# Down projection in three passes instead of four, its results added onto residual rows that already lie in the output

## The chip, the cores and the metric

One core of one Trainium2 chip runs the whole program. Times are device microseconds of an execution; a profiled execution has a trace beside its time. TensorE (PE; its weight loads are PEld), VectorE (DVE), ScalarE (ACT), GpSimd (POOL) and SyncE (SP) run their instructions in order, each on its own, and wait for one another by semaphores. DMAs are issued by SP and by POOL and are carried out by the core's 16 DMA engines.

## The reference

One decoder layer in fp32 for 2048 prompt rows of width 1024 and for 32 sample rows (8 requests of 4): a mixer, a cross-attention over a memory, and a feed-forward part, each between two RMS norms. The change lies in the last lines of the last part:

```python
hf = rmsnorm(h, lw['ln_ffn_pre'])
f = (jax.nn.silu(hf @ lw['w_gate']) * (hf @ lw['w_up'])) @ lw['w_down']
h = h + rmsnorm(f, lw['ln_ffn_post'])
```

`w_gate` and `w_up` are 1024 x 2816, `w_down` is 2816 x 1024. What is asked is h of both groups of rows, and the states and memory keys of the parts before.

## The kernel before

From about 860 us on, everything large is one list of passes, and a pass is a list of units: `o` (w_out), `s` (scores), `v` (values), three `g` passes (gate and up, over blocks of 3, 3 and 2 row blocks) and the `d` passes (down). A row block is 256 rows; there are NJ = 8.

A unit of a `d` pass is one row block against one part of w_down. It is computed as seven products instead of eight (sums and differences of the four quarters of the operands are multiplied, and PSUM banks are read in between and then accumulated on). Each product is made of k-tiles of 128, and each k-tile of three matmuls of 128 x 128 by 128 x 512, because both operands are split into an upper half (rounded by ScalarE) and a lower half (the rest, by VectorE). The 22 k-tiles per row are 11 pairs u, and `PARTS` says which pairs a pass takes: 2, 3, 3 and 3. So a product of a pass of n pairs has n x 3 matmuls, and `d` has 11 x 7 x 3 x 8 matmuls in all.

The order in which the products run is `TURN` (0, 1, 3, 2, 5, 4, 6), with product 0 of the next unit ahead of product 6 of this one (`order`). I call such a place in the list a step. In every step the program writes: the product's matmuls, the emptying of its bank (`evac_d`: ACT copies for some products, DVE adds for the others), the upper and lower halves of the moving rows of the step four ahead (`Unit.hi`, on rows `raw` that SP loads from `aT`), one piece of the coming pass's weights where there is one (`Pieces.larger` on ACT, `Pieces.smaller` on DVE), one turn of each pending sequel (`posts`, `tick`), and one turn of a side list (`aux`, by `RATES`). The order of issue on each engine is pinned to the order in which it is written.

The weights of a pass are seven pieces, each the right operand of one product. A piece is loaded in one or two transfers through three staging tiles (`st`, `stage()`), split by ACT and DVE into a ring tile `r0` to `r6`, and the next transfer is issued when a staging tile has been read. In a pass's last unit one transfer's worth is converted per step, and the rest in the first unit of the next pass. Between `d` passes a ring tile `r7` lets two more be converted in the second last unit. Pieces of the `o`, `s` and `v` passes are wide (four k-tiles, `wide`): they use another 4 KB per partition, `e0` to `e6`.

Sums of the passes go through a tensor `yp` in DRAM: `evac_d` stores or accumulates (`accum_op`) each half row block there by a POOL DMA. In the last pass POOL accumulates `yp` into the SBUF tile `y`, `after_down` squares, takes the reciprocal root (`rstd_rows`, one operation of it on POOL), scales (L1730), has POOL accumulate the residual rows from `hX`, and then POOL stores the result. The last two units work otherwise (`after_direct`): their `yp` and `hX` rows are loaded by SP into spare tiles (L2148 to L2153) three units before the end, and DVE adds them.

The samples' rows take part in the gate and up passes as extra columns (`s_f`), and `samples_down` does their down projection as a side list from the first `d` pass on, with weights of its own (44 transfers of 256 KB).

Of the kernel before, what the change touches and what calls it, by code (L numbers as in the profile page):

```python
# [42 lines left out]
def hymba_kernel(ctx: ExitStack, tc: tile.TileContext, a: dict, o: dict, dbg: dict | None = None):  # L43
# [1376 lines left out]
    pg = pd = samp2 = s_f = None  # L1420
# [24 lines left out]
    PARTS = [(0, 2), (2, 3), (5, 3), (8, 3)]  # L1445
# [156 lines left out]
    made, ring = [0], [7, None]  # L1602
    inside, spent = {}, set()

    class Pieces:
# [15 lines left out]
        def larger(self):  # L1621
# [4 lines left out]
            if i not in self.at:  # L1626
                k = made[0] % ring[0]
# [4 lines left out]
                r = (ring[1] if k == 7 else rp).tile([P, 2 * RW], F32R, name=f"r{k}")  # L1632
                if self.wide:

                    e = rx.tile([P, 1024], F32R, name=f"e{k}")
# [139 lines left out]
    def after_rows(j, m, y, ss, ga, x):  # L1775
# [15 lines left out]
        nc.gpsimd.dma_start(out=hX[rows(j, m)], in_=y)  # L1791
# [69 lines left out]

    def evac_gate(sg, w):
# [14 lines left out]
    def evac_up(sg, w, blk, u):  # L1877
# [6 lines left out]
        def ev(name, ps):  # L1884
# [13 lines left out]
            if name == "C21":  # L1898
                nc.gpsimd.dma_start(out=aT[js[0]:js[0] + n, :, u].rearrange("j p c -> p j c"), in_=og.rearrange("p j q c -> p j (q c)"))
        return ev  # L1900

    def after_down(j, m, y):

        add_rows(y, yp[j][:, m * D:(m + 1) * D])
        yield from pause(6)
        ss = small.tile([P, 8], F32, name="sq2", bufs=8)
        for n in range(2):
            nc.scalar.activation(mxt(), half(y)[n], AF.Square, accum_out=ss[:, n:n + 1])
# [8 lines left out]
    def after_direct(j, m, y, ss, h, last):  # L1917

        if not last:
            yield  # L1920
        if last:
            nc.scalar.activation(mxt(), half(y)[0], AF.Square, accum_out=ss[:, 0:1])
            nc.vector.tensor_tensor(half(y)[1], half(y)[1], half(gain["ln_ffn_post"])[1], op=ALU.mult)
            rs = rstd_rows(ss)
            nc.vector.tensor_tensor(half(y)[0], half(y)[0], half(gain["ln_ffn_post"])[0], op=ALU.mult)
            for n in (1, 0):
                t = half(y)[n]
                nc.vector.scalar_tensor_tensor(t, t, rs[:, 0:1], h[n], op0=ALU.mult, op1=ALU.add)
                nc.sync.dma_start(out=o["y"][rows(j, m), n * 512:(n + 1) * 512], in_=t)
            return  # L1930
        rs = rstd_rows(ss)
        yield
        scaled(y, rs, gain["ln_ffn_post"])
        nc.vector.tensor_tensor(y, y, h, op=ALU.add)
        nc.sync.dma_start(out=o["y"][rows(j, m)], in_=y)

    def evac_d(p, j, z, h, last):

        y = {}
        final = p == len(PARTS) - 1  # L1940
        ss = [small.tile([P, 8], F32, name="sq2", bufs=8) for _ in range(2)] if z else None

        def ev(name, ps):
            m, n = divmod(AT[KEEP.get(name, name)], 2)
            if m not in y:
                y[m] = pd.tile([P, D], F32, name="y", bufs=7)
# [10 lines left out]
            end = last and name == "C21"  # L1957
            if z and not end:
                later.append(lambda: nc.scalar.activation(mxt(), t, AF.Square, accum_out=ss[m][:, n:n + 1]))
            if name in ("C12", "C21"):  # L1960
                if z:
                    posts.append(after_direct(j, m, y[m], ss[m], h[m], end))
                elif final:
                    posts.append(after_down(j, m, y[m]))
# [4 lines left out]
    def samples_down():  # L1969

        m = pd.tile([P, D], F32, name="m")[:NS]
        ss = small.tile([P, 8], F32, name="s_sq", bufs=1)
        for n in range(2):
            ps = mxt()

            for k0 in range(0, FT, 4):
                ws = []
                for kt in range(k0, min(k0 + 4, FT)):
                    ws.append(pd.tile([P, 512], F32, name="w", bufs=4))
                    nc.sync.dma_start(out=ws[-1], in_=a["w_down"][n, kt // 2, :, (kt % 2) * 512:(kt % 2 + 1) * 512])  # L1980
                yield from pause(5)
                for g, w in enumerate(ws):
                    kt = k0 + g
                    nc.tensor.matmul(ps[32 * g:32 * g + 32], lhsT=s_f[:, kt].rearrange("p h t -> p (h t)"), rhs=w,
                                     start=kt < 4, stop=kt >= FT - 4, tile_position=(0, 32 * g))
                yield
            t = m[:, n * 512:(n + 1) * 512]
# [3 lines left out]
            yield  # L1991
            nc.vector.tensor_tensor(t, t, half(gain["ln_ffn_post"])[n][:NS], op=ALU.mult)
            yield
        h = pd.tile([P, D], F32, name="y", bufs=7)[:NS]
# [13 lines left out]
    RATES = {"o": (0, 9), "s": (0, 9), "v": (0, 0), "g": (6, 4), "d": (0, 8)}  # L2008
# [23 lines left out]
    def enter(k):  # L2032
# [13 lines left out]
        if kind == "g":  # L2046
            if i == 0:
                rctx.close()
                pg = fctx.enter_context(tc.tile_pool(name="pg", bufs=1, reuse_waits="tile"))
# [256 lines left out]
```

## Time and profile before

| | us |
|---|---|
| median of 3 runs | 2885.15 (2884.6 to 2893.62) |
| profiled execution, its own time | 2880.55 |
| its span, first to last instruction | 2878.6 |
| `d` passes, from the first 128 x 512 matmul after the gate stage (2381) to the end | 497 |

In a table by stretches each engine's busy time stands with the number of its instructions, PEclk is the share of full TensorE clock that was granted in that stretch, and DMA the mean busy share of the 16 engines. Idle time of an engine costs only where TensorE waits for it.

### The profile page before, as it was taken

The numbers are of one execution on the slowest core, as the hardware profiler recorded it, in microseconds if no ns is written. First come the engines' busy times: TensorE is split into PE (matmuls) and PEld (weight loads), VectorE is DVE, ScalarE is ACT, GpSimd is POOL, SyncE is SP. The second block draws the span as 40 slices with busy tenths as digits, with TensorE's granted clock in tenths as the row PEclk, the third lists the DMA queues.
The fourth block names the chain that finished last, engine by engine and source line by source line (L and its number), as shares of the span: only waits on it lengthen the run. The fifth ranks groups of instructions, "written<-read, shape, count | busy, mean of one in ns | idle before, by whom it ended". The sixth has DMA issues, their size and how long they took to land. (4 is left out here: it accounts for less than half of the span.)

```text
span 2878.6 us, 42299 instructions
## 1 busy us (share of the span) xinstructions
PE 2762.0 (96%) x15207; PEld 2369.9 (82%) x15207; DVE 2083.5 (72%) x3915; ACT 1523.0 (53%) x3045; POOL 556.6 (19%) x754
## 2 busy tenths in 40 slices
PE   8999999999988999999899999999999999899996
PEld 8888787787866878878798988889999997677774
DVE  7677677776737887777887787677678886655665
ACT  5545553644446786777754534434455554444452
POOL 2142342321321321025312100001000000011122
PEclk9999999999999999999999999999999999999998
DMA  7345535342256885568855567763243347877787
GB/s 250 117 138 183 150 109 158 107 150 87 78 200 232 278 293 200 173 193 244 270 187 203 172 237 265 244 229 129 106 145 133 125 140 229 249 168 172 177 215 229
DMA packets 161137, 530.02 MB, mean 184 GB/s; under 512 B 19408, under 2 KB 30848, under 8 KB 149408
## 3 DMA queue, kind: packets, MB, share of 16 engines
q1 hardware_dynamic: 99504, 331.81, 35.7%
q0 software_dynamic: 49184, 170.52, 19.2%
q10 hardware_dynamic: 12240, 24.99, 2.6%
q8 instruction: 120, 1.97, 0.3%
q14 instruction: 89, 0.73, 0.1%
HBM read 373.10 MB, written 154.15 MB: 183 GB/s over the span
## 5 line engine op out<-in xcount | busy, mean ns | idle before, releaser
L134 PE MATMUL accA<-r,s 128*128 128x512 f32 (+2 forms) x1792 | 641.9, 358 | 42.3 <-DVE y L1954 12.0
L136 PE MATMUL accA<-r,s 128*128 128x512 f32 (+2 forms) x1792 | 631.8, 353 | 1.9 <-DVE s L1574 1.8
L135 PE MATMUL accA<-r,s 128*128 128x384 f32 (+2 forms) x1600 | 556.2, 348 | 2.0 <-DVE r L1645 2.0
L134 PEld LDWEIGHTS accA<-r,s 128*128 128x128 f32 x1792 | 341.2, 190 | 100.1 <-ACT s L1572 20.9
L1572 ACT ACTIVATE s<-sum 128x512 fp32r<-128x512 f32 (+2 forms) x488 | 289.1, 593 | 233.9 <-DVE sum L1554 105.2
L136 PEld LDWEIGHTS accA<-r,s 128*128 128x128 f32 x1792 | 341.1, 190 | 34.0 <-DVE s L1574 3.4
L134 PE MATMUL accC<-r,s 128*128 128x512 f32 (+2 forms) x896 | 320.9, 358 | 19.2 <-ACT y L1952 7.9
L135 PEld LDWEIGHTS accA<-r,s 128*128 128x128 f32 x1600 | 304.8, 190 | 25.6 <-DVE r L1645 4.6
L1574 DVE TENSOR_TENSOR s<-sum,s 128x512 fp32r<-128x512 f32 (+2 forms) x488 | 310.7, 644 | 20.1 <-ACT s L1572 18.8
L136 PE MATMUL accC<-r,s 128*128 128x512 f32 (+2 forms) x896 | 315.2, 352 | 0.4 <-DVE s L1574 0.3
L1574 DVE TENSOR_TENSOR s<-raw,s 128x512 fp32r<-128x512 f32 (+2 forms) x366 | 234.5, 641 | 71.6 <-ACT s L1572 69.4
L135 PE MATMUL accC<-r,s 128*128 128x384 f32 (+2 forms) x800 | 277.0, 346 | 0.3 <-DVE r L1645 0.3
L1572 ACT ACTIVATE s<-raw 128x512 fp32r<-128x512 f32 (+2 forms) x366 | 218.2, 596 | 67.5 <-PE accC L136 50.0
L128 ACT ACTIVATE whi<-wraw 128x1024 fp32r<-128x1024 f32 (+2 forms) x148 | 137.1, 940 | 186.3 <-PE acc L135 98.4
L134 PEld LDWEIGHTS accC<-r,s 128*128 128x128 f32 x896 | 169.9, 190 | 50.6 <-issue 12.0
L129 DVE TENSOR_TENSOR wlo<-wraw,whi 128x1024 fp32r<-128x1024 f32 (+2 forms) x148 | 163.1, 1112 | 64.3 <-ACT whi L128 63.6
L136 PEld LDWEIGHTS accC<-r,s 128*128 128x128 f32 x896 | 170.0, 190 | 16.6 <-DVE s L1574 1.5
L134 PE MATMUL acc<-xh,whi 128*128 128x512 f32 (+1 forms) x464 | 168.5, 364 | 8.4 <-ACT xh L289 8.2
L142 POOL TENSOR_TENSOR rs<-ms,nhalf 128x1 f32<-128x1 f32 (+4 forms) x125 | 114.9, 920 | 317.9 <-DVE ms L140 301.6
L136 PE MATMUL acc<-xh,wlo 128*128 128x512 f32 (+1 forms) x464 | 164.6, 356 | 1.7 <-DVE wlo L129 1.7
L135 PE MATMUL acc<-xl,whi 128*128 128x512 f32 (+1 forms) x464 | 164.3, 355 | 0.2 <-DVE xl L290 0.2
L135 PEld LDWEIGHTS accC<-r,s 128*128 128x128 f32 x800 | 152.0, 190 | 10.8 <-DVE r L1645 0.6
(649 smaller groups left out, 5835.9 us busy)
## 6 DMA issues: line engine op xcount, KB each, us to landing
raw<-in_w_gu_dram SPq DMA_DIRECT2D x66, 1024.0 KB, 5.0
wraw<-in_w_in_fm_dram SPq DMA_DIRECT2D x52, 512.0 KB, 3.6
wraw<-in_w_in_tm_dram SPq DMA_DIRECT2D x48, 512.0 KB, 3.7
yp<-y POOLq DMA_DIRECT2D x48, 512.0 KB, 7.3
raw<-aT SPq DMA_DIRECT2D x24, 768.0 KB, 5.1
st<-in_w_down_dram SPq DMA_DIRECT2D x34, 512.0 KB, 6.4
aT<-og POOLq DMA_DIRECT2D x22, 768.0 KB, 4.1
hX<-y POOLq DMA_DIRECT2D x32, 512.0 KB, 6.6
```

The lines of the kernel that those rows point to most:

```text
L128: last[0] = nc.scalar.activation(hi[:, cs], raw[:, cs], AF.Copy)
L129: nc.vector.tensor_tensor(lo[:, cs], raw[:, cs], f(hi)[:, cs], op=ALU.subtract)
L134: nc.tensor.matmul(ps, lhsT=wh, rhs=ah, start=start, stop=False, skip_group_check=more)
L135: nc.tensor.matmul(ps, lhsT=wh, rhs=al, start=False, stop=False, skip_group_check=more)
L136: nc.tensor.matmul(ps, lhsT=wl, rhs=ah, start=False, stop=stop, skip_group_check=more)
L142: nc.gpsimd.tensor_tensor(out=rs[:rows, :cols], in0=ms[:rows, :cols], in1=nhalf[:rows, :cols], op=ALU.pow)
L1572: nc.scalar.activation(h3, v, AF.Copy)
L1574: return lambda: nc.vector.tensor_tensor(l3, v, f(h3), op=ALU.subtract)
```

## The change

- `PARTS` becomes 3, 4 and 4 pairs: three `d` passes instead of four, the last two with wide pieces (16 KB per partition with both halves), whose `e` tiles come from a new pool `rd`, opened before the last gate pass. The ring is seven tiles throughout; `r7` and the two early pieces are gone.
- In the value pass the residual rows are stored to the output `y` itself instead of `hX`, for all row blocks but the last. In the last `d` pass the result is accumulated there by one POOL DMA.
- In the last pass the tiles `y` begin as rows of `yp`, which SP loads one unit ahead; every bank is then emptied by a DVE add. Nothing is accumulated into SBUF any more.
- Only the last unit reads residual rows into staging tiles (`after_last`).
- `samples_down` joins the side list in the last gate pass, loads 22 transfers of 512 KB into `e` tiles, and waits for the columns `s_f` that a product needs (`there`).

```diff
-    PARTS = [(0, 2), (2, 3), (5, 3), (8, 3)]
+    PARTS = [(0, 3), (3, 4), (7, 4)]
...
-        nc.gpsimd.dma_start(out=hX[rows(j, m)], in_=y)
+
+        nc.gpsimd.dma_start(out=(hX if x is not None or j + 1 == NJ else o["y"])[rows(j, m)], in_=y)
...
-        add_rows(y, yp[j][:, m * D:(m + 1) * D])
-        yield from pause(6)
...
-        add_rows(y, hX[rows(j, m)])
-        yield from pause(5)
-        nc.gpsimd.dma_start(out=o["y"][rows(j, m)], in_=y)
...
+        yield
+        nc.gpsimd.dma_start(out=o["y"][rows(j, m)], in_=y, accum_op=ALU.add)
...
+    def after_last(j, m, y, ss, h):
+
+        hy, ga = half(y), half(gain["ln_ffn_post"])
+        if m == 0:
+            nc.vector.tensor_tensor(hy[0], hy[0], ga[0], op=ALU.mult)
+            yield
+            nc.vector.tensor_tensor(hy[1], hy[1], ga[1], op=ALU.mult)
+        else:
+            nc.scalar.activation(mxt(), hy[0], AF.Square, accum_out=ss[:, 0:1])
+            nc.vector.tensor_tensor(hy[0], hy[0], ga[0], op=ALU.mult)
         rs = rstd_rows(ss)
...
+        for n in (1, 0):
+            nc.vector.scalar_tensor_tensor(hy[n], hy[n], rs[:, 0:1], half(h)[n], op0=ALU.mult, op1=ALU.add)
+            nc.sync.dma_start(out=o["y"][rows(j, m), n * 512:(n + 1) * 512], in_=hy[n])
...
-            if name in KEEP or name == "C21":
-                if z:
-                    nc.vector.tensor_tensor(t, ps, half(z[m])[n], op=ALU.add)
-                else:
-                    nc.scalar.copy(t, ps)
+            if not final and (name in KEEP or name == "C21"):
+                nc.scalar.copy(t, ps)
             else:
                 nc.vector.tensor_tensor(t, ps, t, op=ALU.add)
...
+                    w = f(rd.tile([P, 1024], F32R, name=f"e{2 * (i % 3) + c}"))
+                    nc.sync.dma_start(out=w, in_=a["w_down"][n, u])
...
+            while us[-1] >= there[0]:
                 yield
...
-    RATES = {"o": (0, 9), "s": (0, 9), "v": (0, 0), "g": (6, 4), "d": (0, 8)}
+    RATES = {"o": (0, 9), "s": (0, 9), "v": (0, 0), "g": (6, 4), "d": (0, 10)}
...
+            if i + 1 == len(BLOCKS):
+                aux.append(samples_down())
...
+        if i == 2 and n + 1 < len(work) and passes[work[n + 1][0]][:2] == ("d", len(PARTS) - 1):
+
+            ys[n + 1] = {}
+            for m in range(2):
+                ys[n + 1][m] = pd.tile([P, D], F32, name="y", bufs=6)
+                nc.sync.dma_start(out=ys[n + 1][m], in_=yp[work[n + 1][1]][:, m * D:(m + 1) * D])
...
-        p = coming if work[cur][2] == 1 or coming and kind == "d" and work[cur][2] == 2 and i in (5, 4) else now if begins[cur] else None
+        p = coming if work[cur][2] == 1 else now if begins[cur] else None
```

SP's order at the program's end before: five units' `aT` rows, then the last two units' addends, then the last unit's `aT` rows, then stores.

```order
L1595 DMA raw<-aT 128x1536 x5
L2148 DMA r_27114<-yp 128x1024
L2153 DMA r_27114<-hX 128x1024
L2148 DMA r_27114<-yp 128x1024
L2153 DMA m<-hX 128x1024
L2148 DMA st<-yp 128x1024
L2153 DMA st<-hX 128x1024
L2148 DMA st<-yp 128x1024
L2151 DMA w<-hX 128x512 x2
L1595 DMA raw<-aT 128x1536
L1935 DMA out_y_dram<-y 128x1024 x3
L1929 DMA out_y_dram<-y 128x512 x2
```

The same place now: one pair of `yp` rows per unit, between the `aT` rows, and the residual rows of the last unit only.

```order
L2169 DMA y<-yp 128x1024 x2
L1599 DMA raw<-aT 128x2048
L2169 DMA y<-yp 128x1024 x2
L1599 DMA raw<-aT 128x2048
L2169 DMA y<-yp 128x1024 x2
L2157 DMA st<-hX 128x1024 x2
L1934 DMA out_y_dram<-y 128x512 x4
```

The eight addends no longer stand ahead of the last `aT` rows, and no `aT` load is left behind the last two pairs.

POOL in the last pass before, for two half row blocks:

```order
L1721 DMA y<-yp 128x1024
L1721 DMA y<-hX 128x1024
L1915 DMA out_y_dram<-y 128x1024
L142 TENSOR_TENSOR rs<-ms,nhalf 128x1
L1721 DMA y<-yp 128x1024
L1721 DMA y<-hX 128x1024
L1915 DMA out_y_dram<-y 128x1024
L142 TENSOR_TENSOR rs<-ms,nhalf 128x1
```

And now, for two half row blocks:

```order
L142 TENSOR_TENSOR rs<-ms,nhalf 128x1
L1919 DMA out_y_dram<-y 128x1024
L142 TENSOR_TENSOR rs<-ms,nhalf 128x1
L1919 DMA out_y_dram<-y 128x1024
```

Of three POOL DMAs per half row block one is left; it accumulates.

DVE at the end of the program now (`y<-acc` empties a bank; L1925, L1927, L1930 and L1954 multiply by the gain; L1933 closes a row half):

```order
L1949 TENSOR_TENSOR y<-accC,y 128x512
L1925 TENSOR_TENSOR y<-y,ga 128x512
L1949 TENSOR_TENSOR y<-accA,y 128x512
L1954 TENSOR_TENSOR y<-y,ga 128x512
L1927 TENSOR_TENSOR y<-y,ga 128x512
L1729 TENSOR_TENSOR sq_27100<-sq_26966 128x1
L140 TENSOR_SCALAR ms<-sq_27100 128x1
L1933 SCALAR_TENSOR_TENSOR y<-y,rs,st 128x512 x2
L1949 TENSOR_TENSOR y<-accA,y 128x512
L1930 TENSOR_TENSOR y<-y,ga 128x512
```

The first half row block's closing operations stand before the add that empties the last bank.

## Rows read from the trace of the kernel before

**Rows 1.** The page's head and its first part: busy time, share of the span and instructions of an engine.

```profile
span 2878.6 us, 42299 instructions
PE 2762.0 (96%) x15207; PEld 2369.9 (82%) x15207; DVE 2083.5 (72%) x3915; ACT 1523.0 (53%) x3045; POOL 556.6 (19%) x754
```

**Rows 2.** The table by stretches: stretch and its length, busy time of each engine (instructions), granted clock, DMA share, GB/s. In this order: entry into the `d` passes, their three changes of pass, the inside of the last pass, its last three units, the tail, the inside of the `o` pass, the changes from `o` to `s` and from `s` to `v`.

```profile
2360.00:2392.00 32.00, 27.37 (x160) 24.53 (x158) 26.73 (x50) 18.29 (x34) 1.28 (x2) 0.89 0.58 192
2452.00:2490.00 38.00, 30.27 (x117) 22.60 (x115) 27.44 (x46) 21.66 (x40) 2.13 (x4) 0.87 0.79 272
2580.00:2622.00 42.00, 34.75 (x138) 26.96 (x138) 29.41 (x46) 23.12 (x39) 3.46 (x4) 0.93 0.77 203
2716.00:2746.00 30.00, 24.18 (x102) 18.40 (x101) 19.89 (x32) 16.42 (x28) 1.79 (x3) 1.00 0.78 216
2746.00:2820.00 74.00, 74.00 (x328) 61.21 (x327) 52.06 (x102) 39.23 (x93) 25.55 (x35) 1.00 0.96 238
2820.00:2868.60 48.60, 32.87 (x122) 24.74 (x120) 27.49 (x51) 13.58 (x37) 10.97 (x16) 0.89 0.79 224
2868.60:2878.60 10.00, 0.00 (x0) 0.00 (x0) 5.95 (x9) 0.72 (x2) 0.87 (x1) 0.66 0.36 144
905.00:1040.00 135.00, 134.89 (x643) 112.04 (x642) 106.41 (x186) 99.64 (x214) 43.30 (x67) 1.00 0.76 264
1040.00:1080.00 40.00, 36.56 (x164) 29.31 (x164) 36.70 (x53) 34.42 (x65) 10.22 (x12) 0.96 0.90 305
1232.00:1250.00 18.00, 16.01 (x71) 12.07 (x70) 14.44 (x23) 14.93 (x33) 2.02 (x3) 1.00 0.46 167
```

**Rows 3.** Waits of TensorE from 2381 us to the end: who waited for whom, us in total, times, longest.

```profile
PE accA L134 <- DVE y L1954: 12.0, 5, 5.4
PE accC L134 <- ACT y L1952: 7.9, 5, 3.3
```

**Rows 4.** ScalarE's upper halves of weight pieces (L1641), 2440 to 2746 us: its idle time before them, by what ended it (us, times).

```profile
  DMA st<-wT: 22.8, 14
  DMA st<-in_w_down_dram: 8.3, 3
```

**Rows 5.** The chain that ended last, in order of time, near the end: start, us, what.

```profile
2816.73 26.16 DMA raw<-aT
2842.99 0.53 ACT s L1572
```

**Rows 6.** DMA from 2740 us to the end: queues with packets, MB and share of the 16 engines (q0 is POOL's, q1 SP's), then issues with their count, KB each and median us to landing.

```profile
q0 software_dynamic: 5222, 18.97, 59.1%
q1 hardware_dynamic: 3051, 11.33, 22.6%
...
y<-yp POOLq DMA_DIRECT2D x12, 512.0 KB, 8.7
y<-hX POOLq DMA_DIRECT2D x12, 512.0 KB, 8.3
out_y_dram<-y POOLq DMA_DIRECT2D x12, 512.0 KB, 8.7
raw<-aT SPq DMA_DIRECT2D x6, 768.0 KB, 7.1
...
st<-yp SPq DMA_DIRECT2D x2, 512.0 KB, 24.9
```

**Rows 7.** The timeline of TensorE at a group of the samples' matmuls: start, us, engine, line, operation, tiles, shape, count.

```profile
2392.07 1.06 PE L1984 MATMUL mx<-w,s_f 128*32 128x512 f32 x8
```

**Rows 8.** VectorE's timeline where the samples' rows are closed.

```profile
2582.16 1.27 DVE L1232 SCALAR_TENSOR_TENSOR m<-m,rs,y 32x1024 f32<-32x1024 f32 x1 [4.34 <-DMA y<-hXs]
```

**Rows 9.** DMA issues of 2452 to 2490 us: count, KB each, median us to landing.

```profile
st<-wT SPq DMA_DIRECT2D x4, 512.0 KB, 6.8
...
st<-wT SPq DMA_DIRECT2D x4, 256.0 KB, 4.4
```

**Rows 10.** Groups of VectorE's instructions inside the `o` pass, 905 to 1040 us: line, operation, tiles, shapes, count, busy us, mean ns of one, idle before.

```profile
L1574 DVE TENSOR_TENSOR s<-sum,s 128x512 fp32r<-128x512 f32 x26 | 17.8, 686 | 0.6 <-ACT s L1572 0.6
L1730 DVE SCALAR_TENSOR_TENSOR y<-y,rs,ga 128x1024 f32<-128x1024 f32 x13 | 16.6, 1277 | 0.0
...
L1554 DVE TENSOR_TENSOR sum<-raw 128x512 f32<-128x512 f32 x12 | 8.3, 688 | 0.2
L1750 DVE TENSOR_TENSOR y<-accB,y 128x512 f32<-128x512 f32 x7 | 4.8, 691 | 4.1 <-PE accB L136 4.1
```

**Rows 11.** The timeline of the tail, the last product of TensorE first.

```profile
2866.30 0.47 PE L134 MATMUL accA<-r,s 128*128 128x512 f32 x1 [0.88 <-DVE sq L1725]
...
2868.20 0.39 PE L136 MATMUL accA<-r,s 128*128 128x512 f32 x1
2868.62 0.69 DVE L1950 TENSOR_TENSOR y<-accA,st 128x512 f32<-128x512 f32 x1 [2.22 <-PE accA L136]
2869.23 1.28 DVE L1730 SCALAR_TENSOR_TENSOR y<-y,rs,ga 128x1024 f32<-128x1024 f32 x1
...
2870.54 1.23 DVE L1934 TENSOR_TENSOR y<-y,st 128x1024 f32<-128x1024 f32 x1
...
2872.78 0.87 POOL L142 TENSOR_TENSOR rs<-ms,nhalf 128x1 f32<-128x1 f32 x1 [5.08 <-DVE ms L140]
2873.69 1.42 DVE L1928 SCALAR_TENSOR_TENSOR y<-y,rs,w 128x512 f32<-128x512 f32 x2 [0.47 <-POOL rs L142]
```

More of the change, by code (lines that the diff above doesn't have):

```diff
@@ L1418, in hymba_kernel, with rooms4 @@
     RW = 1536
[L1420 removed]
+    pg = pd = samp2 = s_f = rd = None
+    def rooms4():
+        return rd or rx
     posts = []
@@ L1859, in after_values @@
         put(4, u, 0)
+    there = [0]
     def evac_gate(sg, w):
@@ L1898, in ev, with after_down @@
             if name == "C21":
+                if w > n * P:
+                    there[0] = u + 1
                 nc.gpsimd.dma_start(out=aT[js[0]:js[0] + n, :, u].rearrange("j p c -> p j c"), in_=og.rearrange("p j q c -> p j (q c)"))
         return ev
-    def after_down(j, m, y):
-        add_rows(y, yp[j][:, m * D:(m + 1) * D])
-        yield from pause(6)
-        ss = small.tile([P, 8], F32, name="sq2", bufs=8)
-        for n in range(2):
-            nc.scalar.activation(mxt(), half(y)[n], AF.Square, accum_out=ss[:, n:n + 1])
+    def after_down(j, m, y, ss):
         yield
@@ L1912, in after_down, with evac_d @@
         scaled(y, rs, gain["ln_ffn_post"])
-        add_rows(y, hX[rows(j, m)])
-        yield from pause(5)
-        nc.gpsimd.dma_start(out=o["y"][rows(j, m)], in_=y)
-    def after_direct(j, m, y, ss, h, last):
-        if not last:
-            yield
[L1921 to L1930, printed above, removed]
-        rs = rstd_rows(ss)
[L1932 to L1939, printed above, removed]
+        yield
[4 more added lines that the diff above has]
+            nc.vector.tensor_tensor(hy[0], hy[0], ga[0], op=ALU.mult)
+            yield
+            nc.vector.tensor_tensor(hy[1], hy[1], ga[1], op=ALU.mult)
+        else:
+            nc.scalar.activation(mxt(), hy[0], AF.Square, accum_out=ss[:, 0:1])
+            nc.vector.tensor_tensor(hy[0], hy[0], ga[0], op=ALU.mult)
+        rs = rstd_rows(ss)
+        for n in (1, 0):
+            nc.vector.scalar_tensor_tensor(hy[n], hy[n], rs[:, 0:1], half(h)[n], op0=ALU.mult, op1=ALU.add)
+            nc.sync.dma_start(out=o["y"][rows(j, m), n * 512:(n + 1) * 512], in_=hy[n])
+    def evac_d(p, j, y, h):
         final = p == len(PARTS) - 1
-        ss = [small.tile([P, 8], F32, name="sq2", bufs=8) for _ in range(2)] if z else None
+        ss = [small.tile([P, 8], F32, name="sq2", bufs=8) for _ in range(2)] if final else None
         def ev(name, ps):
@@ L1956, in ev @@
                 return
-            end = last and name == "C21"
-            if z and not end:
+            if h and name == "C22":
+                nc.scalar.activation(mxt(), t, AF.Square, accum_out=ss[m][:, n:n + 1])
+                nc.vector.tensor_tensor(t, t, half(gain["ln_ffn_post"])[n], op=ALU.mult)
+            elif final and not (h and name == "C21"):
                 later.append(lambda: nc.scalar.activation(mxt(), t, AF.Square, accum_out=ss[m][:, n:n + 1]))
             if name in ("C12", "C21"):
-                if z:
-                    posts.append(after_direct(j, m, y[m], ss[m], h[m], end))
+                if h:
+                    posts.append(after_last(j, m, y[m], ss[m], h[m]))
                 elif final:
-                    posts.append(after_down(j, m, y[m]))
+                    posts.append(after_down(j, m, y[m], ss[m]))
                 else:
@@ L2078, in before_loads @@
     def before_loads(k):
+        nonlocal rd
         kind, i, _ = passes[k]
-        if kind != "d":
+        if kind != "g" or i + 1 < len(BLOCKS):
             drain(aux)
```

87 lines of the change are left out of this document (42 added, 45 removed).

## The prediction

> **What bounds the kernel now.** I read the page's head first: TensorE is busy 2762.0 of 2878.6 us [rows 1], so the time can only fall where TensorE stands still or runs at half clock. The change touches the last projection, so next came a table by stretches of it [rows 2]. The stretch 2746 to 2820, inside a pass, is solid: 74.00 us busy of 74 at clock 1.00. The stretches around the four changes of weights and the end are not. I price each as its length less busy time times granted clock, since a busy microsecond at the lower level (1.2 of 2.4 GHz) does half the work:
>
> entry from the gate stage, 2360 to 2392: 32 - 27.37 x 0.89 = 7.6 us;
> first change of pass, 2452 to 2490: 38 - 30.27 x 0.87 = 11.7;
> second, 2580 to 2622: 42 - 34.75 x 0.93 = 9.7;
> third, 2716 to 2746: 30 - 24.18 = 5.8;
> last three units, 2820 to 2868.6: 48.6 - 32.87 x 0.89 = 19.3;
> tail without a matmul: 10.0.
>
> Together 64.1 us. Then the waits of TensorE in that stage [rows 3]: at changes of pass it waits for VectorE and ScalarE to empty PSUM (12.0 and 7.9 us), and those stand behind weight pieces that have not landed: ScalarE idled 22.8 and 8.3 us before a piece's upper half [rows 4]. Near the end it is one transfer: the last unit's aT rows, issued at 2816.73, landed 26.16 us later [rows 5], where the median of its kind is 7.1 us [rows 6].
>
> Why 26 us: over 2740 to 2879 the software queue (POOL's DMAs) holds the 16 engines 59.1% and the hardware queue 22.6% [rows 6]. That is 82.1 us for 36 POOL transfers of 512 KB, 2.28 us each, and 31.4 us for 11.33 MB, 1.45 us per 512 KB. A unit of the last pass there takes two reads of yp, two of hX and two writes, all POOL's, and 768 KB of aT: 6 x 2.28 + 1.5 x 1.45 = 15.9 us of DMA. It has 7 x 9 matmuls; with 74 us for 328 of them [rows 2], 0.226 us each, that is 14.2 us. The pass asks more of the DMA engines than it lasts, the backlog grows, and the two units' addends loaded ahead of the last aT rows (24.9 us to landing, rows 6) meet it.
>
> **The change part by part.**
> The matmuls stay: 11 x 7 x 3 x 8 = 1848, 417 us, however they are cut. So do the samples' 44: a group of four holds TensorE 1.06 us [rows 7], and by the order of instructions 4 of 12 groups move into the gate stage and the rest into the first pass. Neutral there; they no longer end beside the second change of pass, where VectorE stood 4.34 us for hXs [rows 8]. What they may cost now (a fold in the first unit, the same hXs wait in the first pass at 2.0-us steps): 0 to 4 us, taken as 1, as a step's bank wait hides most of it.
>
> One change of pass goes. The three left each convert 14 pieces, seven of them in the last unit of the pass before, with three in flight.
> Entry: now 14 pieces (512 and 256 KB) instead of 7, but one step later each product needs two. The seven done ahead cover the first three products; after that the steps shrink from 2.7 to 2.0 us. Bounds 5 (the third change now, of the same shape with a start two steps earlier, 5.8) and 12 (the first, 11.7); I take 7, near the entry of now.
> First change, three to four units deep: the outgoing unit's steps are 2.0 us as now, the incoming 2.7. Bounds 4.9 (the change from w_out to the wide scores' weights, 40 - 36.56 x 0.96, the same wide pieces) and 11.7; I take 6, nearer to the wide one, because a wide piece's 512 KB takes 6.8 us [rows 9], and three in flight on 2.7-us steps cover 8.1.
> Second, wide to wide: the attention stage does it twice, at 4.9 and 2.0 us [rows 2]; upper bound the 9.7 of today. I take 4.
>
> The end: a unit of the last pass now moves 1 MB of aT, two loads of yp on SP's queue and two accumulating stores: 2 x 2.28 + 4 x 1.45 = 10.4 us of DMA in 7 x 12 x 0.226 = 19.0 us, 55% instead of 112%. With no backlog the aT rows land in about the 7.1 us of their kind and nothing else is late: VectorE, which takes over the adds that ScalarE's copies did, has 7 adds of 0.69, 7 lower halves of 0.69, 4 sums of 0.69 and 2 scalings of 1.28 [rows 10], 15.0 us of 19.0. The first attention pass, 905 to 1040, ran the same steps with VectorE busy 106.41 of 135 us (79%) and TensorE 134.89 [rows 2]: such a load hides. What is left of 19.3 us: bounds 0 and 10 (half of it, if the adds delay PSUM), taken as 1.5, mostly the last product's wait for its bank, 0.88 us now [rows 11].
> POOL loses 24 accumulating loads and 16 yp stores; it is on no path but the one above. The moved residual rows (hX to the output) are the same store.
>
> Tail: of today's 10.0 us, VectorE's scaling and addend of another row half (1.28 and 1.23) stand before the final row [rows 11]. After, the other half's two closing operations (1.42 for both) stand before the last PSUM add instead, and one gain product has been done earlier. From the last matmul: add 1.9, square 2.8, POOL's power 4.2, two closing operations 5.7, then 3.5 from there to the end as now: 9.3. Bounds 7 and 10.
>
> Sum of what stays: 1 + 7 + 6 + 4 + 1.5 + 9.3 = 28.8, so 64.1 - 28.8 = 35.3 us are saved: 2880.55 - 35 = 2845 for the profiled execution. The median shown, 2885.15, is 4.6 above that execution; the forecast is 2846. With all low bounds (0, 5, 4.9, 2, 0, 7) 18.9 stay: 2835. With all high ones (4, 12, 11.7, 9.7, 10, 10) 57.4 stay: 2874, and 2878 on the median's footing.
>
> A rule against the change: the Trainium skill, Perfetto Trace Analysis, DMA Optimizations, says that smaller transfers may let some work start sooner. The trace agrees in part: 256-KB pieces land in 4.4 us, 512-KB ones in 6.8 [rows 9]. By it the wider pieces would make each change of pass late, which is the first rival.
>
> **The rivals.**
> First: the changes of pass keep their price (12 + 11.7 + 9.7 instead of 17): every piece is 512 KB, 2.4 us later than half of today's, and ScalarE, in order, holds PSUM copies behind it. Against it the attention stage, with the same pieces at 4.9 and 2.0. Time 2846 + 16 = 2862.
> Second: VectorE bounds the last pass. In the two steps of a unit that hold a scaling it has 0.69 + 0.69 + 0.69 + 1.28 = 3.35 us against 2.7; if no other step gives it back, 0.65 x 2 x 8 = 10 us: 2856. Against it 905 to 1040, with two whole-row operations per half.
> Third, slower: the rows' six buffers are three units; the load for a unit waits until the accumulating store three units before has landed, and SP's queue, with the next aT rows behind it, waits too. From that store's issue (the fifth step of the following unit) to the use there are ten steps, 27 us, of which the load takes some 8.7: it decides when a store takes over 18 us. The median is 8.7 [rows 6], but 24.9 and 26 us have been seen in this pass. At 31 us five units wait 13 us each: 2846 + 65 = 2911.
> Fourth, no change: the backlog stays (the stores are still POOL's, and weights and rows now meet in one place) and the changes of pass keep their price: 2846 + 16 + 18 = 2880.
>
> **How the numbers follow.** Forecast 0.62 (its own range 2835 to 2858), first rival 0.17, second 0.08, fourth 0.07, slower 0.06. The range 2833 to 2868 takes in the first two rivals. A change under 0.3% (8.7 us) can't be told from none: faster 0.87, same 0.07, slower 0.06.
>
> **What would show it.** Three changes of pass, each losing under 8 us, after stretches at clock 1.00; aT rows of the last unit landing under 10 us; no DMA slice at 99% through the last pass; TensorE solid there with VectorE near 80%. It is wrong if TensorE waits for y's adds in every unit of the last pass, if SP waits for accumulating stores, or if ScalarE's idle time before pieces stays at 31 us.

## The result and the profile after

The changed kernel's median is 2856.2 us over 4 runs (2854.98 to 2863.87); the kernel before, timed beside it, 2884.88 (2883.42 to 2893.62). The ratio is 0.99, interval 0.9874 to 0.9926: 28.7 us less, where 39 were forecast; the time lies inside the range of 2833 to 2868. The profiled execution has a span of 2853.3 us instead of 2878.6.

The page's head after:

```profile
span 2853.3 us, 41834 instructions
PE 2757.0 (97%) x15207; PEld 2362.4 (83%) x15207; DVE 2074.9 (73%) x3820; ACT 1486.6 (52%) x2926; POOL 526.2 (18%) x716
```

TensorE has the same 15207 matmuls as in [rows 1] and is busy 5 us less, at a mean granted clock of 0.99 instead of 0.986; most of the gain is idle time that has gone.

The table by stretches after, columns as in [rows 2]: entry into the `d` passes, the fold of the samples' sums in the first unit, first change of pass, second change, inside of the last pass, last units, tail.

```profile
2372.00:2405.00 33.00, 27.77 (x167) 24.43 (x168) 26.64 (x48) 19.73 (x36) 0.71 (x1) 0.90 0.63 212
2470.00:2490.00 20.00, 18.73 (x83) 15.15 (x82) 13.74 (x25) 7.06 (x15) 2.20 (x4) 1.00 0.32 105
2518.00:2545.00 27.00, 25.32 (x107) 19.48 (x106) 24.43 (x32) 17.43 (x25) 1.94 (x3) 1.00 0.84 274
2684.00:2714.00 30.00, 25.45 (x97) 19.68 (x96) 21.73 (x31) 12.77 (x22) 1.43 (x2) 0.89 0.76 235
2714.00:2835.00 121.00, 121.00 (x525) 98.27 (x525) 89.78 (x152) 42.77 (x94) 18.47 (x26) 1.00 0.62 151
2801.00:2843.00 42.00, 41.13 (x179) 33.13 (x177) 30.26 (x52) 13.35 (x30) 5.76 (x9) 1.00 0.51 123
2843.30:2853.30 10.00, 0.33 (x2) 0.00 (x0) 4.34 (x8) 0.72 (x2) 0.76 (x2) 0.66 0.28 106
```

Priced as in the prediction (length less busy time times clock):

| place | before | forecast | after |
|---|---|---|---|
| entry | 7.6 | 7 | 8.0 |
| samples' fold | - | 1 | 1.3 |
| changes of pass | 11.7, 9.7, 5.8 | 6, 4 | 1.7, 7.3 |
| last units | 19.3 | 1.5 | 0.9 |
| tail | 10.0 | 9.3 | 9.7 |
| sum | 64.1 | 28.8 | 28.9 |

(The tail is counted from the end of the last matmul, as before; its row begins 0.33 us ahead of that.) The largest entry went: the last units lose 0.9 us instead of 19.3.

TensorE's waits after, 2381 us to the end, as in [rows 3]:

```profile
PE accA L134 <- DVE t L1902: 4.7, 1, 4.7
PE accC L134 <- ACT s L1576: 3.8, 1, 3.8
PE accA L134 <- DVE y L1949: 1.9, 2, 1.0
```

The first is the entry, the second the second change of pass; the third, two waits of at most 1.0, is all that TensorE waits for the adds into `y`. The 12.0 and 7.9 us of before are gone.

The DMA from 2714 us to the end, queues and issues as in [rows 6]:

```profile
q0 software_dynamic: 1986, 7.22, 33.4%
q1 hardware_dynamic: 3024, 12.58, 25.1%
...
out_y_dram<-y POOLq DMA_DIRECT2D x13, 512.0 KB, 5.5
raw<-aT SPq DMA_DIRECT2D x5, 1024.0 KB, 5.1
y<-yp SPq DMA_DIRECT2D x10, 512.0 KB, 6.5
```

POOL's queue holds a third of the engines instead of 59.1%, and `aT` rows of 1 MB land in 5.1 us, where the last 768 KB of before took 26.16 [rows 5].

Why the trace's own gain is 25.3 and not 35 is seen at one landmark, the first matmul that waits at the entry of the `d` passes (TensorE's timeline). Before:

```profile
2378.36 0.59 PE L134 MATMUL accA<-r,s 128*128 128x272 f32 x1 [4.13 <-DVE t L1894]
```

After:

```profile
2391.48 0.59 PE L134 MATMUL accA<-r,s 128*128 128x272 f32 x1 [4.73 <-DVE t L1902]
```

From there to the end the kernel is 500.2 - 461.8 = 38.4 us shorter, but it arrives there 13.1 us later, and 38.4 - 13.1 = 25.3. Of the 13.1, 0.6 is the longer wait in the bracket, and 5.0 had gathered by the 9000th matmul, ahead of the last gate pass. The other 7.5 come from the samples' four groups that moved there. Counted between the same neighbouring matmuls in both kernels, the groups' slots are 1.4, 2.9, 2.9 and 1.2 us, 8.4 together, of which 0.9 is won back elsewhere in that stage. The two long ones have a wait of this kind (the same timeline, after):

```profile
2234.02 1.05 PE L1993 MATMUL mx<-e,s_f 128*32 128x512 f32 x2 [0.67 <-DVE s_f L1905]
```

The group asks for columns `s_f` that VectorE writes in the same step. The wait is 0.67 us, and the last product then runs 1.05 us by itself instead of beside the other three: such a place costs 1.7 us more than a slot of 1.2.

### The profile page after: what moved, and what is told of

The parts are those of the page before. It is cut to its first block, busy times and chain, and to the rows that moved or that the text cites. A ratio compares the mean times of both kernels' runs of the same rounds, so it can differ in the third digit from the quotient of the medians.

```text
span 2853.3 us, 41834 instructions
## 1 busy us (share of the span) xinstructions
PE 2757.0 (97%) x15207; PEld 2362.4 (83%) x15207; DVE 2074.9 (73%) x3820; ACT 1486.6 (52%) x2926; POOL 526.2 (18%) x716
## 5 line engine op out<-in xcount | busy, mean ns | idle before, releaser
L135 PE MATMUL accA<-r,s 128*128 128x384 f32 (+2 forms) x1472 | 504.8, 343 | 1.9 <-DVE r L1649 1.9
L134 PEld LDWEIGHTS accA<-r,s 128*128 128x128 f32 x1792 | 340.6, 190 | 86.3 <-issue 17.7
L1576 ACT ACTIVATE s<-sum 128x512 fp32r<-128x512 f32 (+1 forms) x456 | 282.3, 620 | 217.1 <-DVE sum L1558 92.1
L136 PEld LDWEIGHTS accA<-r,s 128*128 128x128 f32 x1792 | 340.2, 190 | 34.2 <-DVE s L1578 2.8
L1578 DVE TENSOR_TENSOR s<-sum,s 128x512 fp32r<-128x512 f32 (+1 forms) x456 | 305.6, 677 | 21.6 <-ACT s L1576 21.2
L135 PEld LDWEIGHTS accA<-r,s 128*128 128x128 f32 x1472 | 280.2, 190 | 21.3 <-DVE r L1649 5.0
L1578 DVE TENSOR_TENSOR s<-raw,s 128x512 fp32r<-128x512 f32 (+1 forms) x342 | 232.3, 679 | 52.5 <-ACT s L1576 50.7
L1576 ACT ACTIVATE s<-raw 128x512 fp32r<-128x512 f32 (+1 forms) x342 | 213.3, 624 | 72.0 <-PE accC L136 53.8
L135 PE MATMUL accC<-r,s 128*128 128x384 f32 (+2 forms) x736 | 250.5, 340 | 0.3 <-DVE r L1649 0.3
L134 PEld LDWEIGHTS accC<-r,s 128*128 128x128 f32 x896 | 168.9, 189 | 37.4 <-ACT sg L1877 5.3
L136 PEld LDWEIGHTS accC<-r,s 128*128 128x128 f32 x896 | 169.1, 189 | 16.2 <-DVE s L1578 0.9
L134 PE MATMUL accB<-r,s 128*128 128x512 f32 (+2 forms) x448 | 157.6, 352 | 0.0
```

Source lines behind the costliest of these rows:

```text
L134: nc.tensor.matmul(ps, lhsT=wh, rhs=ah, start=start, stop=False, skip_group_check=more)
L135: nc.tensor.matmul(ps, lhsT=wh, rhs=al, start=False, stop=False, skip_group_check=more)
L136: nc.tensor.matmul(ps, lhsT=wl, rhs=ah, start=False, stop=stop, skip_group_check=more)
L1576: nc.scalar.activation(h3, v, AF.Copy)
L1578: return lambda: nc.vector.tensor_tensor(l3, v, f(h3), op=ALU.subtract)
```

## The experiments

Two questions were open: what had made the end stall, and what of the gain belongs to which part of the change. My reading after the result was that the eight addends of the last two units, issued by SP in one burst onto nearly full DMA engines, made the stall, and that the fewer passes are a gain of their own. The rival was the prediction's own cause: the last pass asks for more DMA than it lasts, so a backlog grows whatever stands at its end.

SP's timeline of the kernel before, near the end:

```profile
2801.96 0.32 SPq L1595 DMA_DIRECT2D raw<-aT  x1
2802.39 0.67 SPq L2148 DMA_DIRECT2D r<-yp  x1
...
2809.37 4.12 SPq L2151 DMA_DIRECT2D w<-hX  x2
2816.73 0.32 SPq L1595 DMA_DIRECT2D raw<-aT  x1
```

The DMA issues of the kernel before from 2746 to 2802, ahead of the burst (count, KB each, median us to landing):

```profile
y<-yp POOLq DMA_DIRECT2D x8, 512.0 KB, 8.1
raw<-aT SPq DMA_DIRECT2D x5, 768.0 KB, 6.8
```

The `aT` rows land after 5.1, 4.2, 6.8, 7.5 and 7.4 us in turn, and POOL's twelve transfers from 2774 to 2802 after 7.9 to 9.0. The times rise once, when POOL's sums begin, and then stay: no backlog grows. The burst's transfers then land after 10.8, 13.6, 15.8 and so on up to 27.6 us, and the `aT` rows behind them after 26.16.

**The changed kernel once more** (after_again), nothing edited.

> The changed kernel unchanged, as the mark that the variants of this batch are compared with, and for a second trace of it. In its first trace the passes ahead of the gate stage, where no instruction differs, ran 5 us later than in the trace of before. If that is chance between executions, the second trace has another figure (-3 to +3 us); if the change of addresses or of the residual rows' destination makes it, it is 4 to 6 us again. Time 2852 to 2860 either way.

Measured: 2854.55 us median of 5, ratio 0.9906 (0.989 to 0.9922), span 2850.7. The landmark stands at 2388.71, so the `d` passes take 462.0 us, as in the first trace to 0.2. At the 9000th matmul this trace is 1.7 us behind that of before, where the first was 5.0: these 3.3 us are chance between executions of one kernel. Whether the remaining 1.7 are is open, as there is one trace of before; the other variants stood between 1.1 ahead of it (four_pool) and 8.2 behind (extra_four) at that place. One thing in these traces speaks against chance alone. From the 6000th matmul (1152 us) to the 9000th, the ten traces of kernels that store residual rows to `y` fall back by 1.3 to 3.3 us against the trace of before, and the two of kernels that store them to `hX` as before (pool_sums, four_pool) by -1.1 and 0.0. The new destination may thus cost some 2 us; no run changes it alone, so that isn't shown.

**Four passes again** (four_passes), with the rest of the change.

```diff
-    PARTS = [(0, 3), (3, 4), (7, 4)]
+    PARTS = [(0, 2), (2, 3), (5, 3), (8, 3)]
```

> PARTS as before (2, 3, 3, 3), everything else of the change kept: one change of pass more, none wide. Theory (the four entries and changes cost 34.8 us in the trace of before by length less busy time times clock, and 17.0 now, so about half of what the change gains comes from them; the end costs under 2 us whatever the number of passes, since a unit of the last pass would take 2 x 2.28 + 3.5 x 1.45 = 9.6 us of DMA in 14.2): 13 to 19 us slower than the changed kernel, 2869 to 2875. Rival (the end made the whole gain, the changes of pass move with other things): within 4 us of the changed kernel.

Measured: 2870.26 us, ratio 0.9958 (0.9944 to 0.9972): 15.7 us above the changed kernel timed beside it. Its waits of TensorE in the `d` passes:

```profile
PE accC L134 <- ACT r L1645: 8.8, 1, 8.8
PE accA L134 <- DVE y L1949: 6.9, 5, 2.1
PE accC L134 <- ACT y L1947: 6.0, 3, 4.4
```

These are the changes of pass: the last alone holds 8.8 us. With the rest of the change in place the three passes are worth some 16 us, and the other parts together with four passes some 12 (0.42%).

**POOL sums the last pass again** (pool_sums): three passes, but `yp` and `hX` are accumulated into `y` by POOL as before, and rows are loaded ahead for the last unit alone, so without a burst.

```diff
+        add_rows(y, yp[j][:, m * D:(m + 1) * D])
+        yield from pause(4)
...
-        nc.gpsimd.dma_start(out=o["y"][rows(j, m)], in_=y, accum_op=ALU.add)
+        add_rows(y, hX[rows(j, m)])
+        yield from pause(3)
+        nc.gpsimd.dma_start(out=o["y"][rows(j, m)], in_=y)
```

> Three passes as in the change, but in the last pass POOL accumulates yp and then hX into y and stores y, as before; only the last unit has its yp rows loaded ahead, as in the change. The two pauses of the sequel are 4 and 3 steps (6 and 5 before), since the steps are longer and there are six tiles y. A unit then asks 6 x 2.28 + 2 x 1.45 = 16.6 us of DMA in 19.0, 87%. Theory (the stall at the end came from a DMA demand above 100%): no stall of 19 us comes back; 0 to 6 us slower than the changed kernel, the last units' aT rows land in 6 to 12 us. Rival (POOL's way through SBUF itself makes the end late, whatever the load): 15 to 25 us slower, with the wait near the end.

Measured: 2855.7 us, ratio 0.9903 (0.989 to 0.9917), no different from the changed kernel. Its table by stretches from the last pass on:

```profile
2714.00:2800.00 86.00, 86.00 (x373) 69.79 (x373) 53.43 (x88) 39.59 (x85) 27.18 (x36) 1.00 0.90 217
2800.00:2832.00 32.00, 31.12 (x134) 24.68 (x132) 19.79 (x36) 12.15 (x30) 9.22 (x13) 1.00 0.84 215
2832.00:2846.60 14.60, 0.04 (x1) 0.00 (x0) 5.45 (x9) 0.72 (x2) 2.87 (x5) 0.63 0.58 181
```

DMA at 84 to 90% stalls nothing, and the tail is 14.6 us instead of 9.7, since POOL's last sums and stores stand in it; what it loses there it has back elsewhere, at the second change of pass among others (a wait of 2.4 us instead of 4.4 in after_again). With three passes and no burst, the new way of summing is worth nothing that can be measured. Three passes with POOL's sums and the burst of addends were not tried.

**The samples' part late** (samples_late): it joins the side list at the first `d` pass.

```diff
-            if i + 1 == len(BLOCKS):
-                aux.append(samples_down())
...
+            aux.append(samples_down())
```

> The samples' part joins the side list at the first down pass, as before; all else of the change kept. The gate stage loses 4 groups of sample matmuls (5.2 us) and two waits of 1.0 us for columns that were written just before; the down passes get the 5.2 us back. Theory (the move is neutral or costs the 2 us of these waits): -3 to +2 us against the changed kernel, as long as the closing of the samples stays clear of a change of pass. Rival (moving them up is worth something, since their closing then falls beside the first change of pass again): 4 to 10 us slower.

Measured: 2859.26 us, ratio 0.9923 (0.991 to 0.9935), 4.7 above after_again (the intervals overlap) and more than expected: the size of the rival, but not by the closing that it named. The two waits for `s_f` are gone, and the landmark stands at 2380.67 instead of 2388.71. But the list must be through by a certain unit, and there the last three groups now run with no step's matmuls between them (TensorE's timeline, the last two groups):

```profile
2488.89 5.07 PE L1993 MATMUL mx<-e,s_f 128*32 128x512 f32 x12 [4.31 <-DMA e<-in_w_down_dram]
```

TensorE waits 4.31 us for the list's weights and then runs 5.8 us at a granted clock of 0.50. From the landmark to the end this kernel takes 475.6 us instead of 462.0. Moving the part up costs 8.4 us in the gate stage, and leaving it late is still no better.

**The next unit's rows a unit earlier** (rows_early): at the second change of pass two loads of `yp` stand beside the weight pieces; here the last pass's first pair is loaded one unit sooner.

```diff
-        if i == 2 and n + 1 < len(work) and passes[work[n + 1][0]][:2] == ("d", len(PARTS) - 1):
+        for n1 in [q for q in (n + 1, n + 2) if i == 2 and q < len(work) and passes[work[q][0]][:2] == ("d", len(PARTS) - 1) and q not in ys and (q == n + 2) == begins[q]]:
```

> The changed kernel with one edit: the first unit's yp rows of the last pass are loaded one unit earlier, so that these two transfers of 512 KB no longer stand among the weight pieces of the second change of pass. In both traces of the changed kernel this change of pass cost 7.3 us (second one 4.6 us of waits and half clock) where 4 were forecast, and the last pieces before it took 9.7 us to land. Theory (the two loads crowd the pieces out): the longest wait there falls from 4.4 to under 2.5 us, 2 to 4 us in time, as in the run with POOL's sums (2.4 us there). Rival (three pieces in flight are too few whatever stands beside them): no difference beyond 1 us. Ratio to before 0.989 to 0.990 against 0.9906.

Measured: 2853.19 us, ratio 0.9883 (0.9863 to 0.9902), no clear difference. TensorE still waits 3.97 us there. The chain of the changed kernel at this change, then that of rows_early:

```profile
2677.74 9.22 DMA st<-in_w_down_dram
2686.98 1.07 ACT r L1645
...
2692.55 1.04 ACT r L1645
2693.59 0.53 ACT s L1576
2694.12 0.77 PE accC L134
```

```profile
2676.33 9.87 DMA st<-in_w_down_dram
```

The weight piece lands as late (9.87 instead of 9.22 us) without the two loads. So these loads don't crowd it; what does is open: the 1-MB `aT` rows and POOL's stores of `yp` stood there in both. Nor does the landing alone set the price: in pool_sums the piece at this place lands after 9.53 us, and the wait is 2.4.

**More load without a burst** (extra_one, extra_four): one, then four more accumulating POOL transfers per unit of the last pass, into a scratch tensor.

```diff
+    extra = tc.dram_tile([NJ, 4, P, D], F32, name="extra")
...
+        if kind == "d" and b == len(PARTS) - 1 and n + 1 < len(work) and i in (0, 1, 3, 2):
+            nc.gpsimd.dma_start(out=extra[g, i], in_=gain["ln_ffn_post"], accum_op=ALU.add)
```

> As extra_four, with one more accumulating transfer per unit: 12.6 + 3.4 = 16 of 19.0 us, 84%. Theory of demand against length: within 3 us of the changed kernel, since it stays under 100%. Rival (any more DMA makes the end later, in proportion): 4 to 11 us slower, a quarter of what four cost.

> The changed kernel with four more accumulating POOL transfers of 512 KB per unit in the last pass (the gain's rows into a scratch tensor), the last unit left out; the outputs stay the reference's. By the changed kernel's trace an accumulating store holds the 16 engines 33.4% of 139 us / 13.8 = 3.4 us and another 512 KB 1.45 us, so a unit asks 2 x 3.4 + 4 x 1.45 = 12.6 of its 19.0 us (66%), and 26 us (138%) with the four. Theory (the end stall is DMA demand above what the pass lasts): the backlog grows 7 us per unit, the aT rows near the end land in 20 us or more, TensorE waits again: 15 to 45 us slower than the changed kernel. Rival (POOL's queue or the order of loads made the stall): within 5 us.

Measured: 2857.99 us, ratio 0.9898 (0.9879 to 0.9917), which can't be told from the changed kernel, and 2863.85, ratio 0.9912 (0.9887 to 0.9938). DMA of extra_four from 2714 us to the end, and a wait of SP in its `d` passes:

```profile
q0 software_dynamic: 5472, 19.93, 69.4%
q1 hardware_dynamic: 3372, 13.99, 24.6%
...
raw<-aT SPq DMA_DIRECT2D x5, 1024.0 KB, 9.3
```

```profile
SPq L2170 <- DMA out_y_dram<-y: 54.8, 5, 13.1
```

The engines are full (94% over the stretch), more so than in the kernel before, yet `aT` rows land in 9.3 us and after 2714 TensorE waits only 0.9 and 0.8 us. What extra_four costs lies at the second change of pass, where the first extra transfers meet the weight pieces: a wait of 10.2 us instead of 3.8. Work does pile up behind POOL here: the output's second store of a unit lands after 12.6 us in the first unit and 15.0, 16.8, 17.4 and 18.1 in the next four, and SP waits 54.8 us in all for such stores before it may load `yp` rows. The `aT` rows stay at 8.8 to 10.2 us all the same. So full engines alone don't stall the end, and not even with a queue that grows on POOL's side.

**The burst** (burst), eight transfers of 512 KB issued by SP three units before the end, alone; and **burst and load** (burst_and_four), with the four extra transfers.

```diff
+                if n + 3 == len(work):
+                    for q in range(8):
+                        nc.sync.dma_start(out=burst[q], in_=yp[q // 2][:, q % 2 * D:(q % 2 + 1) * D])
```

> The changed kernel with a burst of eight transfers of 512 KB on SP's queue three units before the end, at the place where the kernel before has its addends (here from yp to a scratch tensor in DRAM; outputs unchanged). The pass there uses 51 to 62% of the DMA engines. Theory B (burst on nearly full engines): at this load the burst takes 8 x 1.45 = 12 us or somewhat more, the next loads land in up to 20 us, and TensorE waits 0 to 6 us. If the burst alone makes the stall: 12 to 20 us slower than the changed kernel.

> Both: the burst, and the four more accumulating POOL transfers per unit of extra_four (the engines then 95% busy). Theory B: now the loads behind the burst land in 25 us or more and TensorE stands 12 to 25 us near the end; time 12 to 25 us above extra_four (ratio 0.9912), that is 0.995 to 1.000. If burst and load only add up: what burst alone costs, 0 to 6 us above extra_four.

Measured: 2856.69 us, ratio 0.9891 (0.9876 to 0.9906); and 2876.46, ratio 0.9962 (0.9949 to 0.9974). The burst alone is free. With the load it is 12.6 us above extra_four (14 by the ratios), and its trace shows the stall of the kernel before again. TensorE's waits of burst_and_four from 2780 us on, and its DMA from 2790 to 2850:

```profile
PE accC L136 <- DVE s L1580: 12.6, 1, 12.6
```

```profile
extra<-ga POOLq DMA_DIRECT2D x8, 512.0 KB, 13.9
out_y_dram<-y POOLq DMA_DIRECT2D x5, 512.0 KB, 11.7
burst<-yp SPq DMA_DIRECT2D x4, 512.0 KB, 29.9
y<-yp SPq DMA_DIRECT2D x4, 512.0 KB, 23.3
raw<-aT SPq DMA_DIRECT2D x1, 1024.0 KB, 24.0
```

By these medians SP's transfers take 23 to 30 us, as in the kernel before, while POOL's own take 12 to 14. The two causes have to meet: at this place neither alone stalls. What was not tried is the same burst issued behind the last `aT` rows, so whether its size or its place ahead of them does it is open.

**The kernel before without its burst** (four_pool): four passes, sums by POOL, rows loaded ahead for the last unit alone (the edits of four_passes and pool_sums together, with pauses of 6 and 5 turns and seven `y` tiles). The moved samples, the ring of seven tiles and the new closing of the last unit stay, so more than the burst differs from the kernel before.

> Four passes with POOL's sums in the last one, as before (yp and hX accumulated into y, plain store, pauses of 6 and 5 steps, seven tiles y), but the last unit alone has rows loaded ahead: SP's burst of eight addends (4 MB) ahead of the last aT rows, which the kernel before has at 2802 us, is gone. Theory A, as the prediction had it (demand of 112% of the pass's length lets a backlog grow): the aT rows near the end land in 20 us or more and TensorE stands some 15 us, about what before lost. Theory B, formed since (in the trace of before the POOL transfers land in 6.4 to 9.0 us up to 2802, so no backlog grew; the burst on engines that were 96% busy made it): aT rows under 12 us, TensorE waits under 5 us in the last three units. The tail without matmuls is longer by 5 to 12 us in both, since the second last unit's sums now end there. Time by B 2870 to 2882, by A 10 to 15 more.

Measured: 2879.56 us, ratio 0.9976 (0.9964 to 0.9988). Its table by stretches: inside of the last pass, last units, and from the last matmuls' end on.

```profile
2745.00:2820.00 75.00, 75.00 (x332) 62.11 (x331) 52.88 (x104) 40.93 (x99) 25.98 (x38) 1.00 0.96 235
2820.00:2855.00 35.00, 27.08 (x109) 21.00 (x107) 21.84 (x41) 13.02 (x34) 10.77 (x16) 0.93 0.91 239
2855.00:2874.40 19.40, 0.00 (x0) 0.00 (x0) 4.43 (x9) 0.72 (x2) 3.11 (x5) 0.50 0.60 180
```

The last pass is as full of DMA as before (96%), and without the burst the `aT` rows land in 7.2 us (7.0 to 7.3 from the third unit on) and no wait of TensorE after 2745 exceeds 3.2. Its last matmul ends at 2851.3 us, 17 earlier than before, of which 3 were there ahead of the burst's place. But 13 of these go to the tail, which is 23.1 us long, since POOL's accumulations and stores of the last rows stand there. The burst of the kernel before had bought its short tail with the stall; the change has neither.

**Mended** (mended): rows_early, the samples' groups one turn later than their columns, the fold over two steps, and the last add ahead of the other half row's closing operations.

```diff
+            if n == 0:
+                yield
...
-            fold(t, ps)
+            nc.vector.tensor_copy(t, ps[0:32])
+            nc.vector.tensor_tensor(t, ps[32:64], t, op=ALU.add)
+            yield
+            for g in (2, 3):
+                nc.vector.tensor_tensor(t, ps[32 * g:32 * g + 32], t, op=ALU.add)
```

> rows_early and three small edits at places where the trace of the changed kernel shows a wait: a sample group waits one more turn after its columns are written (2 waits of 1.0 us), the samples' fold of 2.8 us is split over two steps (one wait of 1.3 us), and in the last step the add that empties the last bank stands before the other half's closing operations (1.4 us). Each term as it stands in the trace: 2 + 1.3 + 1.3 and the 2 to 4 of rows_early, 6 to 8 us faster than the changed kernel, ratio 0.988. If the waits only move (the next step is late instead), 0 to 3 us.

Measured: 2850.8 us (2850.52 to 2855.39), ratio 0.9877 (0.9858 to 0.9897), the lowest of all, but not the 6 to 8 us that were expected. The waits for `s_f` and at the fold are gone (the four groups now take 4.1 us instead of 8.4), but the wait at the second change stays at 4.7 us, one of 1.1 is new, and the tail is shorter by 0.2, which is less than unedited tails differ (9.1 to 10.2 in these runs). It stands 2.4 us under rows_early on the same chip; its interval overlaps that of the changed kernel, so that it is faster is likely and not settled.

From the landmark to the end, which leaves out what gathers ahead of it, the traces take 500.2 us (before), 461.8 and 462.0 (changed), 477.0 (four_passes), 461.6 (pool_sums), 461.6 (rows_early), 463.0 (extra_one), 468.5 (extra_four), 461.3 (burst), 482.2 (burst_and_four), 489.5 (four_pool) and 461.4 (mended). Burst_and_four stands 13.7 above extra_four there, and nearly all of mended's gain lies ahead of the landmark.

## Why the prediction was right or wrong

**Right: the sum and what the end was worth.** 28.8 us of loss were to stay in the `d` passes and 28.9 did. The last pass is solid: TensorE is busy 121 of 121 us at clock 1.00 and VectorE 74%, so the second rival (VectorE bounds it) did not come. The aT rows land in 5.1 us, as the forecast asked (under 10).

**Wrong: the cause of the stall at the end.** "The pass asks more of the DMA engines than it lasts, the backlog grows" was the step. Landings did not grow ahead of the burst, extra_four with engines at 94% has no stall there, and with four passes and POOL's sums, the engines as full as before, there is none once the burst is gone (four_pool). What makes it is the burst on full engines (burst 0, load and burst 12.6 us of wait). My demand per unit had been worked out from the time that packets took in a full stretch, and that time is no constant: a POOL transfer of 512 KB took 2.28 us of all engines there; in the changed kernel, 33.4% of 139 us for 13.8 transfers is 3.4, and in extra_four 2.7. Nor does a share near 1 mean that no more can be moved. Before, ahead of the burst and within it:

```profile
2774.00:2788.00 14.00, 14.00 (x63) 11.62 (x62) 10.08 (x19) 7.84 (x19) 5.65 (x8) 1.00 0.99 236
2816.00:2830.00 14.00, 11.19 (x50) 8.94 (x48) 8.99 (x18) 4.42 (x11) 5.20 (x7) 1.00 1.05 320
```

The share is 0.99 and then 1.05, and the engines move 236 and then, with the burst's plain loads among the rest, 320 GB/s. A sum of such times over 100% is then no sign of a growing queue. The forecast for this term held by luck: the change removes the burst as well as the load.

**Wrong in parts: the changes of pass.** Forecast 6 and 4, measured 1.7 and 7.3 (4.4 us of wait in the second trace). The total was right and the two sizes were not. ScalarE's upper halves of weight pieces, 2500 to 2714 us, answer to [rows 4]:

```profile
  DMA st<-in_w_down_dram: 8.7, 4
  DMA st<-wT: 1.0, 3
```

31.1 us of idle time before became 9.7, 5.8 of them at the first change (2500 to 2600), where TensorE lost 1.7, and 4.1 at the second. I had bounded both changes by those of the attention stage, which were no guide to which is late: at the second change a piece takes 9.22 us, and TensorE waits for the upper half of its moving rows, which ScalarE writes behind that piece and two more (2693.59 in the chain above). The first rival (each change keeps its price, 33 us with the entry) falls: 17.0. By the rule that I had weighed (the Trainium skill, Perfetto Trace Analysis, DMA Optimizations: smaller transfers may let work start sooner) the wider pieces would be late everywhere. The first change speaks against it, 11.7 to 1.7 us with wider pieces (though its steps are longer and the samples' closing has moved, so the pieces are not tried alone); the second, 7.3 us, lies between the 9.7 and 5.8 of the last two of before and decides nothing.

**Wrong: the samples' move as neutral.** The four groups cost 8.4 us in the gate stage, in both traces of the changed kernel, not 4 x 1.06. I counted the group's own matmuls alone; a slot is 1.2 us, and two hold 1.7 more, as they wait for columns written in the same step. In the `d` passes the four leave 4 x 1.2 = 4.8 us, so the move costs 3.6 where it was to cost nothing. In mended, a turn later, they take 4.1.

**Wrong: the footing.** I set the saving of 35 against the profiled execution and then added 1 us, though I had noted that the median stood 4.6 above it. 2885.15 - 35.3 is 2849.9, and against that the measured 2856.2 is 6.3 too long: 3.6 from the samples, some 1.7 in the `d` passes (38.4 us shorter, where 35.3 and the four groups' 4.8 make 40.1), and the rest within what executions scatter, or from the residual rows' destination, which I had called the same store.

**The tail** came out at 9.7 for a forecast of 9.3 (whose own terms, 5.7 and 3.5, make 9.2). TensorE's last matmul and what follows, answering to [rows 11]:

```profile
2843.23 0.40 PE L136 MATMUL accA<-r,s 128*128 128x512 f32 x1
2843.55 1.42 DVE L1933 SCALAR_TENSOR_TENSOR y<-y,rs,st 128x512 f32<-128x512 f32 x2 [0.75 <-POOL rs L142]
2844.88 0.68 DVE L1949 TENSOR_TENSOR y<-accA,y 128x512 f32<-128x512 f32 x1
```

The two closing operations do stand before the last add, as forecast. In mended they stand behind it, and that gave 0.2 us, within the scatter of tails.

**The other rivals.** The third (SP waits for accumulating stores) had its mechanism but not its price: SP's waits for the output's stores into `y`'s tiles are these, in all, times and longest:

```profile
SPq L2169 <- DMA out_y_dram<-y: 3.2, 5, 1.5
```

3.2 us, and no `aT` row was late by it. In extra_four the same wait is 54.8 us, up to 13.1 at a time, and the `aT` rows still left every 19.4 us. The fourth (no change) needed the stall and the old price of the changes; neither is there.

## What to carry to other kernels

Before a stall is put down to DMA demand, look at each transfer's landing time in order: flat landings up to one place, and long ones behind it, speak of a burst and not of a backlog. Loads that are wanted late are best spread, a few per unit, as long as they stay ahead of their use; in this kernel a burst was free on engines with room and cost 12.6 us of wait on full ones. When side work is moved into a stage that is solid, count its whole slot in the engine that bounds the stage, with the change of operand and the wait for what is written in the same step.

## What was not expected of the hardware

On full DMA engines SP's and POOL's transfers fare differently. In burst_and_four the burst's eight SP transfers landed after 12.5 to 32.6 us and POOL's extra ones, issued from 2787 to 2812 beside them, after 12.1 to 19.1; without the burst (extra_four, same stretch) POOL's took 11.6 to 17.7. There the burst delayed the queue that it stood in and hardly the other; in the kernel before, POOL's transfers rose with it as well, from 7.9 to 9.0 us to 9.9 to 15.6 (issued from 2803 to 2831). And the engine time that a packet takes is no constant: 2.28 us per POOL transfer of 512 KB in the kernel before, at 82% of the engines, 2.7 in extra_four at 94%, and 3.4 in the changed kernel at 59%. These differ in kind too (in the kernel before two in three accumulate into SBUF and the third is a plain store; in the others nearly all accumulate into DRAM), and what makes the difference was not tried.
